# Four value columns of the MLP up-projection as block products in two units, with a shared bank and sums made by transfers

## Chip, cores and metric

The kernel runs on one core of one Trainium2 chip. The metric is the device time of one execution in microseconds (us), as the median of several runs. Engines are named as the profile names them: PE (TensorE, matmul), PEld (its weight loads), DVE (VectorE), ACT (ScalarE), POOL (GpSimd), SP (the queue from which most transfers are issued). PSUM is the memory that matmuls write; a bank is a tile of 128 x 512 f32 in this kernel.

## What is computed

Two decoder layers over 512 tokens of width 1024, in f32. Layer 0 mixes tokens by window attention and a short convolution, layer 1 by gated linear attention. Both then run the gated MLP below, which the change is about, and a per-layer embedding.

```python
D_MODEL, SEQ, D_FF, FFN_CONV_K = 1024, 512, 2816, 3

def _conv_ffn(h, w_up, conv_w, conv_b, w_down):
    u = _causal_depthwise_conv(h @ w_up, conv_w) + conv_b
    gate, up = jnp.split(u, 2, axis=-1)
    return (jax.nn.gelu(gate, approximate=False) * up) @ w_down

def reference(x, p, ...):
    for i in range(DEPTH):
        h = _rms_norm(x, mix_norm[i])
        ...
        x = x + _conv_ffn(_rms_norm(x, ffn_norm[i]), ffn_w_up[i], ffn_conv_w[i], ffn_conv_b[i], ffn_w_down[i])
        x = x + _per_layer_embedding(x, p[i], ple_norm[i], ple_w_gate[i], ple_w_proj[i])
    return x
```

`w_up` has 5632 columns: 2816 gate columns, then 2816 value columns. The convolution has three taps along the tokens.

## The kernel before

**Precision.** An f32 operand is cut into a high and a low part: ACT copies the operand in the reduced format (the high part), DVE subtracts that from the operand (the low part). A product is three matmuls: high x high, high x low, low x high. So each weight tile costs one ACT and one DVE instruction ahead of its matmuls (`cut` at L151 and L153, `cut_blocks` at L861 and L864).

**Column tiles and groups.** The up-projection is computed transposed, 128 columns of `w_up` on the partitions and 512 tokens along the bank. The 22 gate tiles and 22 value tiles of a layer are taken in 11 groups (`for d in range(groups)` in `ffn`): group d holds gate tiles 2d and 2d + 1 and value tiles 2d and 2d + 1.

**A value tile the plain way** (`value`): 8 tiles of 128 rows x 3 matmuls x 2 halves of the tokens, 48 matmuls of 256 columns (lines L177 to L179 inside `mm3`).

**Two gate tiles as block products** (`seven`, L920 on): rows by parity, columns in two tiles, and tokens in two halves form 2 x 2 blocks, and a Strassen-Winograd scheme takes seven block products in place of eight. Each is 12 matmuls (`block_product`, L916 to L918), 84 in all where two plain tiles take 96. The products are W = plain x e1, V = t13 x s1, then plain x o1, t2 x s2, t13 x s3, last x s4 and last x o2. Copies by ACT carry partial sums from one bank to another between them: W goes into the left halves of X and Y (L931, L932), V into a buffer `more` (L938), and two more copies follow (L941, L944). `seven` is a generator; the caller runs other matmuls between its steps. The scheme needs sums of blocks on both sides:
- on the weights, `first_forms` and `more_forms` make them with four DVE operations of 128 x 512 a group (L887, L888, L895, L898), in place in the loaded weights, and cut the results as `t13`, `t2` and `last`;
- on the tokens, `operand` makes s1 to s4 (L833 to L838).

**The order of a group.** PE's order is written out by hand (`manual_schedule(engines={ET.PE})`); the other engines' order comes from a scheduler that works with priorities (`high_priority`) and with explicit orderings (`issue_after`). For group d, PE runs: six eighths of the value tile 2d (`begin`), the gate's W, the rest of that value tile, V and plain x o1 and t2 x s2, the first half of value tile 2d + 1, the gate's t13 x s3, the second half of the value tile, and the gate's last two products. `prepare(d + 1)` issues the next group's loads and cuts. A group has 180 matmuls.

**Loads.** The gate weights of a group (1 MB, L1014) and the next value weights (1 MB, L990) come by SP's queue. Each has one buffer ahead only: the load for group d + 1 waits until the last cut of group d's weights (the `last` cut of `seven`) has read it.

**After the matmuls** (`taps`): DVE scales by the row norm R (L969, or L972 and L976 where `more` is added first), ACT applies the middle tap and the bias (L977), DVE the two other taps (L979, two each). Four tiles a group. Then `close`, in the next group, applies Gelu on ACT (L1130) and multiplies gate and value on DVE (L1034).

**POOL** raises the token norm to its power (`rtok`, L209), once a norm, and issues a few small loads early (L250).

**After the up phase** comes the down phase (`down`), which uses `seven` too, seven times in the whole kernel; the 22 groups of the up phases use it once each.

Of the kernel before, what the change touches and what calls it, by code (L numbers as in the profile page):

```python
# [63 lines left out]
class Kernel:  # L64
# [755 lines left out]
    def operand(self, m, gain, tags):  # L820
# [30 lines left out]
    def cut_blocks(self, src, wide=True, amid=None):  # L851
# [4 lines left out]
        else:  # L856
            h, l = (
                self.sp.tile([P, S + 64], F32R, tag="sq", name=self.nm("t2"), bufs=2)[:, o : o + S] for o in BLOCKS
            )
        h, l = (x.rearrange("p (j n) -> p j n", n=src.shape[2]) for x in (h, l))  # L860
# [5 lines left out]
        n = 2 if wide else 1  # L866
# [53 lines left out]
    def seven(self, od, ws, x, keep=None):  # L920
# [5 lines left out]
        W, V = self.pa(), self.pa()[:, :H]  # L926
        X, Y = self.ps(), self.ps()
        plain, t13, t2 = ws
        left, right = HALVES
# [4 lines left out]
        product(V, t13, 0, x["s1"], True)  # L934
# [14 lines left out]
    def ffn(self, i, project, next_gain):  # L949
# [8 lines left out]
        with tc.tile_pool(name=f"ffn{i}", bufs=1) as fp:  # L958
# [7 lines left out]
            def taps(y, ps, f, more=None, behind=None):  # L966
# [3 lines left out]
                else:  # L970
# [4 lines left out]
                    with tc.issue_after(behind.ins) if behind else nullcontext():  # L975
                        nc.vector.tensor_tensor(z, z, R, ALU.mult)  # L976
# [28 lines left out]

            def prepare(d, behind=None):
# [91 lines left out]
            with tc.manual_schedule(engines={ET.PE}):  # L1098
                late = begin(0, steps, w0c)
                close = lambda: None  # L1100
                for d in range(groups):
# [4 lines left out]
                    V1 = self.pa()  # L1106
                    value(w1c, V1, 0, ND // 2)
                    if d == 0:
                        self.end_norm()
                    copied = next(steps)  # L1110
                    value(w1c, V1, ND // 2, ND)
                    if d == 0:
                        R = self.spread()
# [1183 lines left out]
```

## Time and profile before

| what | us |
|---|---|
| median of 3 runs | 1196.59 (1196.03 to 1197.21) |
| the profiled execution | 1195.99 |
| its span | 1194.0 |
| up phase of layer 0, groups 0 to 10 | 178.4 to about 403 |
| up phase of layer 1 | from about 791.5 to 1018 |
| one group | about 20.45 |

The profile is of one execution; its rows give the start and the duration of an instruction, the engine, the line, the operation, and what it wrote from what. A note in brackets says how long the engine was idle before it, and what ended that. Where a row groups two instructions (x2), its duration covers both. Durations of DVE overlap by some 0.08 us with the next one, so its pace is read from starts. Lines as L864 are those of the kernel before.

### The profile page before, as it was taken

What the parts mean: (1) busy time and instruction counts of PE and PEld (TensorE: products, weight loads), DVE (VectorE), ACT (ScalarE), POOL (GpSimd) and SP (SyncE); (2) the same over time, 40 slices, a digit from 0 to 9 for tenths busy, and PEclk for the clock granted to TensorE, in tenths of its full rate; (3) what the DMA queues carried; (4) which work ended last, traced back from release to release, by engine and by line L of the source; (5) the groups of instructions that cost most, each with busy time, mean ns of one, the idle gap of its engine ahead of it and who ended that gap; (6) DMA issues with size and microseconds to landing.
All of it is one profiled execution on the core that took longest, in us unless ns stands there. A gap on an engine that the chain in (4) does not pass through costs nothing.

```text
span 1194.0 us, 20222 instructions
## 1 busy us (share of the span) xinstructions
PE 1187.1 (99%) x8218; PEld 1079.2 (90%) x8218; DVE 993.3 (83%) x1595; ACT 691.6 (58%) x1138; POOL 46.1 (4%) x64
## 2 busy tenths in 40 slices
PE   9999999999999999999999999999999999999998
PEld 8877789999999988889988988899999999888887
DVE  6786687898999987889879876688989999988595
ACT  7466565656565744756664655555555656655374
POOL 2610000000000000000100000000000000000000
PEclk9999999999999999999999999999999999999999
DMA  7222222333323343422412212223232333323601
GB/s 224 72 97 81 74 89 71 107 107 106 107 93 103 113 137 96 130 73 73 139 59 71 89 54 72 88 76 116 92 116 97 106 107 113 126 89 98 211 1 71
DMA packets 113072, 117.76 MB, mean 99 GB/s; under 512 B 2856, under 2 KB 108002, under 8 KB 112980
## 3 DMA queue, kind: packets, MB, share of 16 engines
q1 hardware_dynamic: 112144, 115.88, 29.8%
q8 instruction: 64, 1.05, 0.4%
q0 software_dynamic: 560, 0.42, 0.3%
q14 instruction: 28, 0.23, 0.1%
q10 hardware_dynamic: 276, 0.18, 0.1%
HBM read 114.37 MB, written 2.10 MB: 98 GB/s over the span
## 4 chain that ended last, share of the span: by engine, by line
PE 88%; DVE 8%; ACT 3%; issue 1%; DMA 0%; POOL 0%; ACTq 0%
PE ps L177 8%; PE ps L178 8%; PE ps L179 8%; PE pa L178 6%; PE pa L179 6%; PE pa L177 6%; PE ps L916 5%; PE ps L918 5%; PE ps L917 5%; PE ps L193 5%; PE ps L191 5%; PE ps L200 4%; PE pa L916 2%; PE pa L918 2%; PE pa L917 2%; DVE wl L864 2%
## 5 line engine op out<-in xcount | busy, mean ns | idle before, releaser
L153 DVE TENSOR_TENSOR wl<-raw,wh 128x1024 fp32r<-128x1024 f32 (+3 forms) x138 | 158.6, 1152 | 39.6 <-ACT wh L151 36.5
L151 ACT ACTIVATE wh<-raw 128x1024 fp32r<-128x1024 f32 (+4 forms) x142 | 140.9, 995 | 68.4 <-PE ps L178 26.3
L861 ACT ACTIVATE wh<-raw 128x1024 fp32r<-128x1024 f32 x90 | 95.7, 1063 | 129.5 <-DVE raw L888 79.0
L979 DVE SCALAR_TENSOR_TENSOR zt<-z,vfa,zt 128x510 f32<-128x510 f32 (+1 forms) x176 | 130.8, 744 | 0.3
L864 DVE TENSOR_TENSOR wl<-raw,wh 128x1024 fp32r<-128x1024 f32 x90 | 109.9, 1221 | 17.5 <-ACT wh L861 16.4
L179 PE MATMUL pa<-b,wl 128*128 128x256 f32 x352 | 97.3, 276 | 0.1
L179 PE MATMUL pa<-a,wl 128*128 128x256 f32 x352 | 97.2, 276 | 0.0
L177 PE MATMUL pa<-a,wh 128*128 128x256 f32 x352 | 97.2, 276 | 0.0
L177 PE MATMUL pa<-b,wh 128*128 128x256 f32 x352 | 97.2, 276 | 0.0
L178 PE MATMUL pa<-a,wh 128*128 128x256 f32 x352 | 97.2, 276 | 0.0
L178 PE MATMUL pa<-b,wh 128*128 128x256 f32 x352 | 97.2, 276 | 0.0
L977 ACT ACTIVATE zt<-z,vfb 128x512 f32<-128x512 f32 x88 | 71.3, 810 | 18.3 <-DVE z L969 8.7
L191 PE MATMUL ps<-b,wh 128*128 128x512 f32 (+1 forms) x192 | 73.0, 383 | 0.0
L193 PE MATMUL ps<-b,wh 128*128 128x512 f32 (+1 forms) x192 | 72.3, 379 | 0.0
L179 PEld LDWEIGHTS pa<-b,wl 128*128 128x128 f32 x352 | 66.1, 188 | 0.3 <-DVE wl L153 0.3
L177 PEld LDWEIGHTS pa<-a,wh 128*128 128x128 f32 x352 | 66.1, 188 | 0.0
L177 PEld LDWEIGHTS pa<-b,wh 128*128 128x128 f32 x352 | 66.1, 188 | 0.0
L178 PEld LDWEIGHTS pa<-b,wh 128*128 128x128 f32 x352 | 66.1, 188 | 0.0
L178 PEld LDWEIGHTS pa<-a,wh 128*128 128x128 f32 x352 | 66.1, 188 | 0.0
L179 PEld LDWEIGHTS pa<-a,wl 128*128 128x128 f32 x352 | 66.1, 188 | 0.0
L916 PE MATMUL ps<-four,wh 128*128 128x256 f32 x232 | 64.7, 279 | 0.0
L918 PE MATMUL ps<-four,wl 128*128 128x256 f32 x232 | 64.1, 276 | 0.0
(532 smaller groups left out, 3711.9 us busy)
## 6 DMA issues: line engine op xcount, KB each, us to landing
raw<-in_ffn_w_up_dram SPq DMA_DIRECT2D x42, 1024.0 KB, 5.1
raw<-in_ffn_w_down_dram SPq DMA_DIRECT2D x13, 1024.0 KB, 5.1
raw<-in_hy_w_in_dram SPq DMA_DIRECT2D x8, 1024.0 KB, 4.9
raw<-in_gla_w_in_dram SPq DMA_DIRECT2D x8, 1024.0 KB, 5.2
raw<-in_ffn_w_down_dram SPq DMA_DIRECT2D x8, 768.0 KB, 4.9
raw<-in_ple_w_gate_dram SPq DMA_DIRECT2D x6, 1024.0 KB, 6.5
raw<-in_hy_w_out_dram SPq DMA_DIRECT2D x16, 256.0 KB, 4.0
raw<-in_gla_w_out_dram SPq DMA_DIRECT2D x4, 1024.0 KB, 5.1
```

The lines of the kernel that those rows point to most:

```text
L151: nc.scalar.activation(hv, v, AF.Copy)
L153: self.rest_cut = nc.vector.tensor_tensor(lv, v, hv.bitcast(F32), ALU.subtract)
L177: mm(out, lh, rh, start=start, stop=False, **kw)
L178: mm(out, lh, rl, start=False, stop=False, **kw)
L179: mm(out, ll, rh, start=False, stop=stop, **kw)
L191: mm(out, lh, rh, start=first, stop=False, **kw)
L193: end = mm(out, lt, rt, start=False, stop=False, **kw)
L861: nc.scalar.activation(h, src, AF.Copy)
L864: nc.vector.tensor_tensor(l, src, h.bitcast(F32), ALU.subtract)
L916: mm(out, wh, xh, start=first and j == 0, stop=False, **kw)
L918: mm(out, wl, xh, start=False, stop=j == ND // 2 - 1, **kw)
L979: nc.vector.scalar_tensor_tensor(out=y[:, tap:], in0=z[:, : S - tap], scalar=w[:, f : f + 1], in1=y[:, tap:], op0=ALU.mult, op1=ALU.add,)
```

## The change

- In `ffn`, `pairs_by_blocks = (1, 4)`: in the groups d = 1 and d = 4, the value tiles 2d + 1 and 2d + 2 form a `Unit` and are computed as seven block products in place of two plain tiles. Its first products (`first`, `second`) stand in PE's order of group d where tile 2d + 1 stood; `third` and `fourth` stand in that of group d + 1 where tile 2d + 2 stood, with `third` ahead of the gate's W and `fourth` after it.
- In `seven`, and in the units, V goes into the right half of W's bank. The product that begins it does so without the start flag.
- Sums on the weight side become additions: the signs of the forms are turned, with `operand` on the token side turned to match and a factor of -1 in `taps`.
- Five sums a layer are made by transfers in `sum_ahead`: a copy of the blocks from DRAM into a tile, then two transfers that add other blocks onto it, all issued by POOL. These are the gate sums of groups 1 and 2 (issued in `prepare(0)`), of group 3 (`prepare(1)`), and the value sums of the two units (each in its own `prepare`). The other forms stay on DVE (`sum_forms`).

Functions that the new code calls and that were there before: `cut_blocks` (now with its body in `cut_into`), `block_product`, `by_parity`, `four`.

```diff
@@ operand
-            nc.vector.tensor_tensor(s12[:, :H], e[:, H:], o[:, H:], ALU.add)
-            nc.vector.tensor_tensor(s12[:, H:], s12[:, :H], e[:, :H], ALU.subtract)
+            nc.vector.tensor_tensor(s12[:, :H], o[:, H:], e[:, H:], ALU.subtract)
+            minus = lambda out, p, q: nc.vector.scalar_tensor_tensor(
+                out=out, in0=p, scalar=-1.0, in1=q, op0=ALU.mult, op1=ALU.subtract
+            )
+            minus(s12[:, H:], s12[:, :H], e[:, :H])
...
-            nc.vector.tensor_tensor(s34[:, H:], o[:, :H], s12[:, H:], ALU.subtract)
+            minus(s34[:, H:], o[:, :H], s12[:, H:])
@@ seven
-        W, V = self.pa(), self.pa()[:, :H]
+        left, right = HALVES
+        W = self.pa()
+        V = W[:, right]
...
-        product(V, t13, 0, x["s1"], True)
+        product(V, t13, 0, x["s1"])
@@ taps
-                        nc.vector.tensor_tensor(z, z, R, ALU.mult)
+                        nc.vector.scalar_tensor_tensor(
+                            out=z, in0=z, scalar=-1.0, in1=R, op0=ALU.mult, op1=ALU.mult
+                        )
@@ ffn
+            pairs_by_blocks = (1, 4)
+            ahead_of = {0: (1, 2), 1: (3,)}
+            blocks = a["ffn_w_up"][i].rearrange("(j u p) n -> u p j n", p=P, u=2)
+            gate_sums, value_sums, places = {}, {}, {}
+
+            def sum_ahead(sums, d, c):
+                key = id(sums)
+                if key not in places:
+                    x = self.four(fp, F32).rearrange("p (h a) b -> p h (a b)", h=2)
+                    places[key] = [x[:, h].rearrange("p (j n) -> p j n", n=2 * P) for h in range(2)]
+                x = sums[d] = places[key][d % 2 if sums is gate_sums else 0]
+                nc.gpsimd.dma_start(x, blocks[0, :, :, c : c + 2 * P])
+                for u in range(2):
+                    nc.gpsimd.dma_start(
+                        x[:, :, u * P : (u + 1) * P], blocks[u, :, :, c + P : c + 2 * P], accum_op=ALU.add
+                    )
+
+            def sum_forms(raw, both13, apart=False):
+                ev, od = self.by_parity(raw)
+                if apart:
+                    b11, b21, b22 = ev[:, :, :P], od[:, :, :P], od[:, :, P:]
+                    plain = self.cut_blocks(raw[:, :, :P])
+                    four = self.four(fp)
+                    h, l = (four[:, 2 * u : 2 * u + 2].rearrange("p a b -> p (a b)") for u in range(2))
+                    t13 = self.cut_into(h, l, both13)
+                    nc.vector.tensor_tensor(b11, b22, both13[:, :, :P], ALU.add)
+                    with tc.high_priority(offset=40):
+                        t2 = self.cut_blocks(b11, False)
+                    nc.vector.tensor_tensor(b21, b21, b11, ALU.add)
+                    return plain, t13, t2
+                plain = self.cut_blocks(raw[:, :, :P])
+                given = both13 is not None
+                if not given:
+                    both13 = ev
+                first, third = both13[:, :, :P], both13[:, :, P:]
+                if not given:
+                    nc.vector.tensor_tensor(first, ev[:, :, P:], ev[:, :, :P], ALU.add)
+                    nc.vector.tensor_tensor(third, od[:, :, P:], ev[:, :, P:], ALU.add)
+                t13 = self.cut_blocks(both13)
+                nc.vector.tensor_tensor(first, od[:, :, P:], first, ALU.add)
+                with tc.high_priority(offset=40):
+                    t2 = self.cut_blocks(first, False)
+                nc.vector.tensor_tensor(od[:, :, :P], od[:, :, :P], first, ALU.add)
+                return plain, t13, t2
+
+            class Unit:
+                def __init__(u, raw, ws):
+                    u.od = self.by_parity(raw)[1]
+                    u.plain, u.t13, u.t2 = ws
+                    u.more = places[id(value_sums)][1].rearrange("p j n -> p (j n)")[:, : S // 2]
+
+                def first(u):
+                    left, right = HALVES
+                    W, u.X, u.Y = self.pa(), self.pa(), self.pa()
+                    self.block_product(W[:, left], u.plain, 0, operands["e1"], True)
+                    for x in (u.X, u.Y):
+                        nc.scalar.copy(x[:, left], W[:, left])
+                    u.V = W[:, right]
+
+                def second(u):
+                    left, right = HALVES
+                    self.block_product(u.V, u.t13, 0, operands["s1"])
+                    nc.scalar.copy(u.more, u.V)
+                    self.block_product(u.X[:, left], u.plain, 1, operands["o1"])
+                    self.block_product(u.Y[:, left], u.t2, 0, operands["s2"])
+                    nc.scalar.copy(u.X[:, right], u.Y[:, left])
+                    u.last = self.cut_blocks(u.od)
+
+                def third(u):
+                    right = HALVES[1]
+                    self.block_product(u.X[:, right], u.t13, 1, operands["s3"])
+                    nc.scalar.copy(u.Y[:, right], u.X[:, right])
+
+                def fourth(u):
+                    left, right = HALVES
+                    self.block_product(u.Y[:, left], u.last, 1, operands["s4"])
+                    self.block_product(u.X[:, right], u.last, 0, operands["o2"])
@@ prepare
-                rv = values.pop()
-                with tc.issue_after(behind.ins) if behind else nullcontext():
-                    w0 = column(rv, rv.shape[2] // P - 1)
+                rv, w0 = values.pop(), None
+                if d - 1 not in pairs_by_blocks:
+                    with tc.issue_after(behind.ins) if behind else nullcontext():
+                        w0 = column(rv, rv.shape[2] // P - 1)
+                if d in pairs_by_blocks:
+                    sum_ahead(value_sums, d, DFF + 256 * d + P)
...
-                ws = self.seven_forms(ev, od, rg)
+                ws = sum_forms(rg, gate_sums.get(d))
                 values.append(load_values(d))
-                return self.seven(od, ws, operands, self.aside), w0, column(values[0], 0)
+                steps = self.seven(od, ws, operands, self.aside)
+                for e in ahead_of.get(d, ()):
+                    sum_ahead(gate_sums, e, 256 * e)
+                if d not in pairs_by_blocks:
+                    return steps, w0, column(values[0], 0)
+                rv = values[0]
+                return steps, w0, Unit(rv, sum_forms(rv, value_sums[d], True))
@@ begin
+                if isinstance(w, Unit):
+                    next(steps)
+                    w.fourth()
+                    return lambda y: taps(y[:, 0], w.Y, NF + 2 * d, w.more)
@@ the loop over groups
+                    unit = w1c if isinstance(w1c, Unit) else None
+                    if unit:
+                        unit.first()
+                        copied = next(steps)
+                        unit.second()
+                        V1 = unit.X
+                    else:
...
                     if d + 1 < groups:
                         steps, w0c, w1c = prepare(d + 1, copied)
-                        cut = self.rest_cut
+                        if unit:
+                            unit.third()
+                            w0c = unit
+                        else:
+                            cut = self.rest_cut
                         late = begin(d + 1, steps, w0c)
```

More of the change, by code (lines that the diff above doesn't have):

```diff
@@ L859, in cut_blocks, with cut_into @@
             )
+        return self.cut_into(h, l, src, amid)
+    def cut_into(self, h, l, src, amid=None):
+        nc = self.nc
+        n = src.shape[1] * src.shape[2] // S
         h, l = (x.rearrange("p (j n) -> p j n", n=src.shape[2]) for x in (h, l))
@@ L865, in cut_blocks @@
         h, l = (x.rearrange("p j n -> p (j n)").rearrange("p (k n) -> p k n", n=P) for x in (h, l))
-        n = 2 if wide else 1
         return lambda j, c: (h[:, n * j + c, :], l[:, n * j + c, :])
@@ L925, in seven @@
         product = self.block_product
-        W, V = self.pa(), self.pa()[:, :H]
+        left, right = HALVES
+        W = self.pa()
+        V = W[:, right]
         X, Y = self.ps(), self.ps()
         plain, t13, t2 = ws
-        left, right = HALVES
         product(W[:, left], plain, 0, x["e1"], True)
@@ L1105, in ffn @@
                         close()
[L1106 to L1113, printed above, removed]
+                    unit = w1c if isinstance(w1c, Unit) else None
[5 more added lines that the diff above has]
+                    else:
+                        V1 = self.pa()
+                        value(w1c, V1, 0, ND // 2)
+                        if d == 0:
+                            self.end_norm()
+                        copied = next(steps)
+                        value(w1c, V1, ND // 2, ND)
+                        if d == 0:
+                            R = self.spread()
                     X, Y, more = next(steps)
```

## The prediction

> **What bounds the kernel now.** I read the page first (busy shares, chain of waits), then busy time by windows, then the timelines of each engine around the changed groups.
>
> ```profile
> span 1194.0 us, 20222 instructions
> PE 1187.1 (99%) x8218; PEld 1079.2 (90%) x8218; DVE 993.3 (83%) x1595; ACT 691.6 (58%) x1138; POOL 46.1 (4%) x64
> PE 88%; DVE 8%; ACT 3%; issue 1%; DMA 0%; POOL 0%; ACTq 0%
> ```
>
> TensorE is never idle for long: a matmul taken out is time gained, unless something else cannot deliver earlier. Who that could be shows by windows (times; busy us and instructions of PE, weight load, DVE, ACT, POOL; clock; DMA share; GB/s):
>
> ```profile
> 301.10:321.60 20.50, 20.50 (x183) 20.50 (x183) 19.08 (x26) 12.15 (x18) 0.00 (x0) 1.00 0.32 105
> 403.40:423.80 20.40, 20.40 (x96) 17.02 (x95) 20.40 (x30) 12.20 (x16) 0.00 (x0) 1.00 0.45 143
> ```
>
> The first is one group of the up phase: DVE has 1.4 us to spare in 20.5. The second opens the down phase: DVE has none. The granted clock is 1.00, and ACT and POOL have room. So the change trades TensorE's time for work of an engine nearly as full, and for transfers.
>
> **What is removed: matmuls.** A unit is 84 matmuls in place of 96; four units save 48. Their pace, from the starts of the first matmul of a block product and of the one after its twelfth:
>
> ```profile
> 224.25 0.28 PE L916 MATMUL pa<-a,wh 128*128 128x256 f32 x1
> ...
> 225.61 0.28 PE L177 MATMUL pa<-a,wh 128*128 128x256 f32 x1
> ```
>
> 12 in 1.36 us, 0.1133 each: 48 x 0.1133 = 5.44 us, 2.72 a layer, 1.36 a unit. The rest asks how late TensorE runs against that schedule. A stall at one place gives the other engines the same time, so the latenesses below are not added within a layer: the largest counts.
>
> **Two products in one bank.** V may now start only when ACT has copied W out twice; in before it had a bank of its own. The second copy and V's first matmul, in the layer's first group and in a steady one:
>
> ```profile
> 185.09 0.33 ACT L932 COPY ps<-pa 128x256 f32<-128x256 f32 x1
> ...
> 185.22 0.28 PE L916 MATMUL pa<-four,wh 128*128 128x256 f32 x1
> ...
> 287.68 0.36 ACT L932 COPY ps<-pa 128x256 f32<-128x256 f32 x1
> ...
> 288.57 0.28 PE L916 MATMUL pa<-four,wh 128*128 128x256 f32 x1
> ```
>
> First group: the copy ends at 185.42, so V is 0.20 late, some 0.25 with a hand-over. Steady: it ends 0.53 ahead, cost nothing; without that cover each of the other groups would pay a part of the copies' 0.62.
>
> **The plain product comes earlier after a unit.** Where a unit ended the group, the next group begins with its plain gate product, without the 36 matmuls of a value column ahead of it, only the unit's third product: 24 matmuls, 2.72 us, sooner. What that product waits for in group 2 of layer 0 is DVE's lower half of the gate weights:
>
> ```profile
> 220.54 1.22 DVE L864 TENSOR_TENSOR wl<-raw,wh 128x1024 fp32r<-128x1024 f32 x1
> ...
> 224.48 0.28 PE L918 MATMUL pa<-a,wl 128*128 128x256 f32 x1
> ```
>
> Ready at 221.76, used at 224.48: 2.72 of slack, and the need moves to just 221.76. Now what goes before it. The load starts when group 1's last cut frees the buffer:
>
> ```profile
> 199.51 0.68 DVE L887 TENSOR_TENSOR raw<-raw 128x512 f32<-128x512 f32 x1
> 200.11 0.68 DVE L969 TENSOR_TENSOR z<-pa,R 128x512 f32<-128x512 f32 x1
> ...
> 203.77 0.75 DVE L979 SCALAR_TENSOR_TENSOR zt<-z,vfa,zt 128x510 f32<-128x510 f32 x1
> 204.43 0.69 DVE L895 TENSOR_TENSOR raw<-raw 128x512 f32<-128x512 f32 x1
> ...
> 211.75 1.22 DVE L864 TENSOR_TENSOR wl<-raw,wh 128x1024 fp32r<-128x1024 f32 x1
> ...
> 212.99 0.37 SPq L1014 DMA_DIRECT2D raw<-in_ffn_w_up_dram  x1
> ...
> 218.99 1.05 ACT L861 ACTIVATE wh<-raw 128x1024 fp32r<-128x1024 f32 x1
> DMA to landing us min/median/max: 4.8/5.0/6.4
> ```
>
> By starts, a 512-wide operation takes 0.60 of DVE and a scaled one 0.66. From the first z of group 1 to that cut, the built order has 23 DVE instructions where before had 20: two gate sums leave, two of the unit's and its t2 cut come, and more taps stand ahead; in all three scaled ones more, +1.98. The sign flips themselves swap a 0.60 for a 0.66, counted in this. Cut 214.95, load +5.0 = 219.97, ACT +1.05, DVE +1.22 = 222.25: late by 0.5, plus what the load loses to the sums' transfers (c).
>
> **c.** The 1 MB load now runs beside unit 4's sum. No row shows an accumulating transfer; the nearest are these (the last line is of POOL's vector loads, 22 KB):
>
> ```profile
> 133.14 1.52 POOL L250 DMA_DIRECT2D vrow<-in_ffn_conv_w_dram  x3 [56.35 <-PE pa L259]
> raw<-in_ffn_w_up_dram SPq DMA_DIRECT2D x42, 1024.0 KB, 5.1
> zt<-in_ffn_w_down_dram SPq DMA_DIRECT2D x6, 512.0 KB, 4.2
> pin<-in_p_dram SPq DMA_DIRECT2D x4, 256.0 KB, 3.6
> DMA to landing us min/median/max: 1.8/2.3/4.9
> ```
>
> 512 KB more costs 5.1 - 4.2 = 0.9. The 512 KB that accumulate beside the load cost nothing if they miss it, and three times that, 2.7, if source, old value and result each count; I take c = 1.0, the price of one passage.
>
> **The sums' own path.** The base copy of group 3's gate sum may start when group 1's t2 cut has read its place (198.91 + 6.74 = 205.7 by the count above). An issue is 0.51; landing I take from SP's rows. Base lands 205.7 + 0.5 + 4.2 = 210.4; POOL waits for it, issues two accumulates (211.4), then unit 4's base, whose place unit 1 gave up at 210.6: lands 216.1; accumulates issued 217.1, landed 220.7. Their reader, ACT's and DVE's cut for unit 4's t13, stands early in the built order: ahead of group 2's t2 cut (0.64) and of the two copies (0.63) that V needs.
>
> ```profile
> 226.97 0.28 PE L916 MATMUL pa<-four,wh 128*128 128x256 f32 x1
> ```
>
> V is due 1.36 earlier than this plus 0.25, at 225.9, so the sum is due at 225.9 - 0.63 - 0.64 - 1.06 = 223.5: 2.8 us of margin, and past it every us is a us of TensorE. Unit 1's sum and the gate sums of groups 1 and 2 have more:
>
> ```profile
> 172.96 1.29 DVE L110 TENSOR_TENSOR four<-four,four 128x512 fp32r<-128x512 f32 x2 [1.08 <-ACT four L109]
> ...
> 189.12 1.23 DVE L864 TENSOR_TENSOR wl<-raw,wh 128x1024 fp32r<-128x1024 f32 x1 [1.46 <-ACT wh L861]
> 193.64 1.04 POOL L209 TENSOR_TENSOR rtok<-rs,mhalf 128x4 f32<-128x4 f32 x1 [58.48 <-DVE rs L208]
> ```
>
> Its place is free at 174.3; base and accumulates land by some 184, its cut comes behind that of 189.12, and POOL is done issuing long before the norm's rtok. Without that cover, rtok, and with it the whole first group's scaling, waits.
>
> On these sums the Trainium skill ("SBUF — State Buffer", section "SBUF: two separate sides") warns that descriptors which GpSimd writes for a DMA are held up while DVE runs an operation in a two-port mode; by that rule the sums would come late as in rival 2. The three POOL loads of 133.14, issued in 0.51 us each, do not bear it out. Its page "DMA: Bandwidth & Descriptors" (section "Anatomy of one DMA — SWDGE (gpsimd) path") gives 2.0 us + bytes / 436e3 for such a DMA; by that estimate the sum lands near 217 and rival 2 has twice the margin to cross.
>
> **Unit 4.** In group 4 the built order puts the Gelu ahead of ACT's copies of the unit's W, and V of the unit waits for those:
>
> ```profile
> 216.88 1.29 DVE L1034 TENSOR_TENSOR u<-zt,zt 128x512 f32<-128x512 f32 x2 [2.47 <-ACT zt L1130]
> ...
> 256.25 1.29 DVE L1034 TENSOR_TENSOR u<-zt,zt 128x512 f32<-128x512 f32 x2 [1.19 <-ACT zt L1130]
> ...
> 272.25 0.28 PE L177 MATMUL pa<-a,wh 128*128 128x256 f32 x1
> ...
> 273.28 1.53 DVE L979 SCALAR_TENSOR_TENSOR zt<-z,vfa,zt 128x511 f32<-128x511 f32 x2
> ...
> 274.90 1.06 ACT L1130 ACTIVATE zt<-zt 128x1024 f32<-128x1024 f32 x1 [1.55 <-DVE zt L979]
> ```
>
> The Gelu is released by the tap that ends at 274.81. Since 198.91 DVE has 0.9 us less to do by then (seven 512-wide fewer, five scaled more). Its idle times before were 2.47, 1.19 and 1.19 = 4.85; now cuts cover one Gelu and part of another (1.35, 0.1, 1.19), and it waits 1.1 + c for the load: 3.75 + c. Release 274.81 - 0.9 - 1.1 + c = 272.8 + c; Gelu, two copies, +1.8: V at 274.6 + c. Due: the unit starts where the old column did (272.25), V 24 matmuls later, less the first unit's gain: 272.25 + 2.72 - 1.36 = 273.6. Late by 1.0 + c = 2.0, the largest of the layer (group 5's load, 2.7 later for DVE's backlog, comes out 0.3 + c late).
>
> **Sum.** 1195.99 - 5.44 + 2 x 2.0 = 1194.55 for the profiled execution (2.0 outside the span, left alone). The runs' median, 1196.59, is 0.60 above it: **1195.1 us**. With c = 0 and no Gelu wait (0.5 a layer) 1192.2; with c = 2.7 it is 1198.5: the forecast's own range.
>
> **Rivals.**
> (1) Nothing is late: the load misses the transfers and DVE gets ahead. For it: PE 99% with 1.4 us of DVE spare. Against: DVE has three operations more ahead of the load. 1195.99 - 5.44 + 0.60 = 1191.2.
> (2) The sums land late, slower than before: place, unit 4's t13 cut in front of group 2's t2 and W copies in both layers. At 1.7 times the landing times assumed (7.1 and 6.1) the path ends 205.7 + 0.5 + 7.1 + 1.0 + 0.5 + 7.1 + 1.0 + 6.1 = 229.0, 5.5 late: 1195.99 - 5.44 + 11.0 + 0.6 = 1202.2; at twice, 1209. It takes over past 225.5 (2.0 late), and ends above before's time past 226.2. For it: POOL's landings reach 4.9 for 22 KB, accumulating was never seen, and DVE is busy. Against: 2.8 us margin.
> (3) DVE becomes the bound: its 2.7 of backlog after unit 4 is not worked off (0.2 a group beyond the Gelu's 1.19) and meets the full window of the down phase. 2.7 + 1.0 late a layer: 1198.6.
> (4) Bank sharing costs in every group: the 0.53 of cover speaks against; 0.3 in 20 more groups gives 1201. Too unlikely for a share of its own.
>
> **Chances.** Forecast 0.44 (0.17 of it below 1194.2), rival 1 0.17, rival 2 0.27, rival 3 0.12 (0.06 of it above 1199.0). A measurement of this kernel can tell some 0.2%, 2.4 us, from no change. Faster 0.17 + 0.17 = 0.34; slower 0.27 + 0.06 = 0.33; same 0.33. The range goes from rival 1 to most of rival 2: 1191.2 to 1201.5.
>
> **What would show it.** Matmuls 48 fewer; a stall of TensorE near 0.2 before the first group's V; in group 2 a wait of 1 to 2 us for the plain weights with the load's landing above 5.0; in group 4 one behind the Gelu; unit 4's accumulates landed near 221. Accumulates landing after 226, or DVE without idle time through groups 5 to 10, would make it wrong to the slow side; no waits at all, to the fast.

## The result, and the profile after

The changed kernel takes 1218.1 us (median of 4 runs, 1216.1 to 1218.62) where the kernel before takes 1196.9 on the same chip: ratio 1.0173, 95% interval 1.0155 to 1.0191. It is slower by 1.7%, 23.0 us above the forecast and outside its range. The profiled execution took 1216.1; its span is 1214.3, 20.3 more than before.

From the page of the changed kernel: the span, the engines' busy time, the chain that ended last by engine, and three rows of DMA issues (count, KB each, median us from issue to landing).

```profile
span 1214.3 us, 20267 instructions
PE 1192.9 (98%) x8170; PEld 1080.3 (89%) x8170; DVE 1001.8 (83%) x1603; ACT 701.5 (58%) x1166; POOL 80.0 (7%) x94
PE 72%; DVE 12%; DMA 6%; issue 6%; ACT 4%; POOL 1%; ACTq 0%; POOLq 0%; DVEq 0%; SPq 0%
raw<-in_ffn_w_up_dram SPq DMA_DIRECT2D x42, 1024.0 KB, 5.0
four<-in_ffn_w_up_dram POOLq DMA_DIRECT2D x10, 512.0 KB, 4.6
four<-in_ffn_w_up_dram POOLq DMA_DIRECT2D x20, 256.0 KB, 6.6
```

PE has its 48 matmuls fewer, but is 5.8 us longer busy, and its idle time grew from 1194.0 - 1187.1 = 6.9 to 21.4. DMA, at 0% of the chain before, now holds 6%. The transfers of 256 KB, the ones that add, land later than the copies of twice their size. The balance of the span: -5.44 for the matmuls taken out, +14.5 of idle PE, and 5.8 + 5.44 = +11.2 because the matmuls that are left keep PE busy for longer; together +20.3.

The idle time by what it waited for (view of PE's waits of the changed kernel: us in total, times, longest):

```profile
PE pa L924 <- ACT wh L870: 4.5, 3, 2.4
PE pa L924 <- ACT ps L941: 4.3, 4, 2.2
PE pa L926 <- DVE wl L873: 2.8, 5, 0.8
PE pa L924 <- ACT pa L1090: 2.1, 2, 1.4
PE ps L924 <- ACT ps L950: 1.0, 2, 0.8
```

Row by row: the plain weights' cut, the copy of W that V waits for in a gate, the lower half of the same weights, the unit's copy that follows its third product, and a copy further on in the scheme of a gate. The median load (5.0) hides it, as a median does: only a few loads are late, those beside the sums and, in group 5 of layer 0, a gate load and a value load beside each other (some 7 us each). Where the time goes shows by windows (times; busy us and count of PE, weight load, DVE, ACT, POOL; clock; DMA share; GB/s), here groups 2 and 5 of layer 0 and all behind group 6 up to the end of that up phase:

```profile
219.30:239.70 20.40, 15.62 (x103) 15.02 (x102) 11.90 (x16) 8.32 (x12) 2.37 (x2) 0.83 0.48 111
...
280.60:301.00 20.40, 17.76 (x145) 16.91 (x145) 14.97 (x20) 10.84 (x19) 0.00 (x0) 1.00 0.31 104
...
321.40:410.00 88.60, 88.60 (x780) 88.40 (x779) 83.63 (x112) 52.06 (x76) 0.00 (x0) 1.00 0.31 100
```

In the first, PE is idle for 4.8 and does 103 matmuls where a full window holds 180; 103 at 0.1133 would be 11.7, not 15.6, so 3.9 more are lost around the waits and to slower matmuls, at a granted clock of 0.83 in the mean. Behind group 6 nothing is lost any more.

Group 2 of layer 0 by rows: first POOL, then DVE and SP's queue, then ACT, then PE (start, us, engine, line, operation; in brackets how long the engine was idle, and what ended that).

```profile
210.23 2.60 POOL L1030 DMA_DIRECT2D four<-in_ffn_w_up_dram  x2 [3.32 <-DMA four<-in_ffn_w_up_dram]
211.75 1.86 POOL L1028 DMA_DIRECT2D four<-in_ffn_w_up_dram  x1
219.09 2.58 POOL L1030 DMA_DIRECT2D four<-in_ffn_w_up_dram  x2 [5.48 <-DMA four<-in_ffn_w_up_dram]
...
213.73 1.22 DVE L873 TENSOR_TENSOR wl<-raw,wh 128x1024 fp32r<-128x1024 f32 x1
215.02 0.37 SPq L1108 DMA_DIRECT2D raw<-in_ffn_w_up_dram  x1
...
222.76 1.06 ACT L870 ACTIVATE wh<-raw 128x1024 fp32r<-128x1024 f32 x1 [3.99 <-DMA raw<-in_ffn_w_up_dram]
...
230.93 1.06 ACT L870 ACTIVATE four<-four 128x1024 fp32r<-128x1024 f32 x1 [5.89 <-DMA four<-in_ffn_w_up_dram]
231.89 0.61 ACT L870 ACTIVATE t<-four 128x512 fp32r<-128x512 f32 x1
232.41 0.36 ACT L940 COPY ps<-pa 128x256 f32<-128x256 f32 x1
232.71 0.33 ACT L941 COPY ps<-pa 128x256 f32<-128x256 f32 x1
```

Group 1's last cut ends at 214.95, and the load leaves at 215.02, just as forecast. But it lands at 222.74, after 7.7 us. Beside it go the second of gate 3's accumulates (landed 217.40; the first landed at 215.00, before the load left), unit 4's base (issued 211.75, landed 218.81, after 7.1) and, from 219.1 on, the next value load and unit 4's accumulates. These land at 229.31 and 230.82. ACT has been idle for 5.89 us by then: its next instruction is the t13 cut of that sum, and the t2 cut and both copies of W stand behind it, all of them with their data ready.

```profile
223.87 0.38 PE L924 MATMUL pa<-a,wh 128*128 128x256 f32 x1 [1.85 <-ACT wh L870]
224.09 0.28 PE L925 MATMUL pa<-a,wh 128*128 128x256 f32 x1
225.13 0.39 PE L926 MATMUL pa<-a,wl 128*128 128x256 f32 x1 [0.76 <-DVE wl L873]
...
226.42 0.41 PE L924 MATMUL pa<-four,wh 128*128 128x256 f32 x1
...
229.41 0.41 PE L926 MATMUL pa<-a,wl 128*128 128x256 f32 x1
...
233.09 0.50 PE L924 MATMUL pa<-four,wh 128*128 128x256 f32 x1 [2.17 <-ACT ps L941]
```

Two waits of PE follow, for the load and for the sum. Between 226.42 and 229.41 stand 14 steps of a matmul in 2.99 us, 0.213 each in place of 0.113. From 233.39 on, behind the second wait, comes another such stretch.

### The profile page after: what moved, and what is told of

Its sections match the earlier page's. It is cut to its first block, busy times and chain, and to the rows that moved or that the text cites. A ratio compares the mean times of both kernels' runs of the same rounds, so it can differ in the third digit from the quotient of the medians.

```text
span 1214.3 us, 20267 instructions
## 1 busy us (share of the span) xinstructions
PE 1192.9 (98%) x8170; PEld 1080.3 (89%) x8170; DVE 1001.8 (83%) x1603; ACT 701.5 (58%) x1166; POOL 80.0 (7%) x94
## 4 chain that ended last, share of the span: by engine, by line
PE 72%; DVE 12%; DMA 6%; issue 6%; ACT 4%; POOL 1%; ACTq 0%; POOLq 0%; DVEq 0%; SPq 0%
PE ps L177 8%; PE ps L178 8%; PE ps L179 7%; PE ps L193 4%; PE ps L191 4%; DMA four<-in_ffn_w_up_dram 4%; PE ps L200 4%; PE ps L924 4%; PE ps L926 4%; PE ps L925 4%; PE pa L178 3%; PE pa L179 3%; PE pa L177 3%; DVE wl L873 3%; DVE zt L990 2%
## 5 line engine op out<-in xcount | busy, mean ns | idle before, releaser
L153 DVE TENSOR_TENSOR wl<-raw,wh 128x1024 fp32r<-128x1024 f32 (+3 forms) x130 | 149.2, 1150 | 36.3 <-ACT wh L151 33.7
L990 DVE SCALAR_TENSOR_TENSOR zt<-z,vfa,zt 128x511 f32<-128x511 f32 (+1 forms) x176 | 129.9, 747 | 1.6 <-ACT zt L988 1.1
L179 PE MATMUL pa<-b,wl 128*128 128x256 f32 x288 | 79.7, 277 | 0.1
L179 PE MATMUL pa<-a,wl 128*128 128x256 f32 x288 | 79.6, 276 | 0.0
L177 PE MATMUL pa<-b,wh 128*128 128x256 f32 x288 | 79.5, 276 | 0.0
L178 PE MATMUL pa<-b,wh 128*128 128x256 f32 x288 | 79.5, 276 | 0.0
L177 PE MATMUL pa<-a,wh 128*128 128x256 f32 x288 | 79.5, 276 | 0.0
L178 PE MATMUL pa<-a,wh 128*128 128x256 f32 x288 | 79.5, 276 | 0.0
L924 PE MATMUL ps<-four,wh 128*128 128x256 f32 x232 | 64.9, 280 | 1.0 <-ACT ps L950 1.0
L925 PE MATMUL ps<-four,wh 128*128 128x256 f32 x232 | 64.1, 276 | 0.0
L179 PEld LDWEIGHTS pa<-b,wl 128*128 128x128 f32 x288 | 54.1, 188 | 0.3 <-DVE wl L153 0.2
L177 PEld LDWEIGHTS pa<-b,wh 128*128 128x128 f32 x288 | 54.1, 188 | 0.0
L178 PEld LDWEIGHTS pa<-b,wh 128*128 128x128 f32 x288 | 54.1, 188 | 0.0
L177 PEld LDWEIGHTS pa<-a,wh 128*128 128x128 f32 x288 | 54.1, 188 | 0.0
L178 PEld LDWEIGHTS pa<-a,wh 128*128 128x128 f32 x288 | 54.1, 188 | 0.0
```

Source lines behind the costliest of these rows:

```text
L153: self.rest_cut = nc.vector.tensor_tensor(lv, v, hv.bitcast(F32), ALU.subtract)
L177: mm(out, lh, rh, start=start, stop=False, **kw)
L178: mm(out, lh, rl, start=False, stop=False, **kw)
L179: mm(out, ll, rh, start=False, stop=stop, **kw)
L924: mm(out, wh, xh, start=first and j == 0, stop=False, **kw)
L925: mm(out, wh, xl, start=False, stop=False, **kw)
```

## Experiments

Line numbers are those of the changed kernel; each diff is against it unless the text names another base.

**Hold unit 4's cut back.** The t13 cut of unit 4 is ordered behind ACT's copy of the gate in hand, so that it can't stand in front of group 2's work.

```diff
-                    t13 = self.cut_into(h, l, both13)
+                    with tc.issue_after(behind.ins) if behind else nullcontext():
+                        t13 = self.cut_into(h, l, both13)
```

> Unit 4's t13 cut is queued on ACT behind group 3's copy, so that nothing of group 2 stands behind the late sum; its transfers run as in the changed kernel. Theory (the wait for the sum in front of group 2's t2 cut and W copies costs its 2.17 and 1.30 us of stall and most of the slow clock after it): those two stalls go, the group 2 load stays late (1.85 and 2.41), 1216.1 falls by 6 to 10, to 1206 to 1210. Rival (DVE's extra work is the bound): other stalls grow in their place, at 1214 or above.

1209.3, ratio 1.0108 (1.0093 to 1.0123): 8 us of the 21 are gone, as expected. V's wait in group 2 is gone in both layers; the wait for the load stays (2.05 + 0.75 in layer 0). So the head of ACT's queue was the one cause, the late load another.

**Another place for unit 4's sum.** It goes to a tile that comes free after group 3's t2 cut, so its transfers move from group 2 to group 4.

```diff
+                if sums is value_sums and d == 4:
+                    x = places[id(gate_sums)][1]
```

> Unit 4's sum goes into the place of group 3's gate sum, which comes free some 35 us later, so its transfers leave groups 1 and 2 altogether. Theory (late sum, and contention on group 2's load, 7.7 and 8.3 us to landing in place of 5.0): load back at 5.0 to 5.5, stalls in group 2 below 0.7 a layer, the stalls in groups 5 and 6 stay: 1216.1 less 16 of group 2 plus 1, 1199 to 1203. Rival (the load is late of itself, DVE's backlog): stall in group 2 stays above 1.5 a layer, 1206 or above.

1225.4, ratio 1.024: a miss, the sum is late in the new place as well. POOL, then ACT in group 4 of layer 0:

```profile
253.03 0.78 POOL L1031 DMA_DIRECT2D four<-in_ffn_w_up_dram  x1 [39.30 <-DVE t L873]
257.24 2.57 POOL L1033 DMA_DIRECT2D four<-in_ffn_w_up_dram  x2 [3.43 <-DMA four<-in_ffn_w_up_dram]
...
267.74 1.06 ACT L870 ACTIVATE four<-four 128x1024 fp32r<-128x1024 f32 x1 [8.66 <-DMA four<-in_ffn_w_up_dram]
```

The base lands after 3.9 (POOL issues again at 257.24), the first accumulate 4.7, and the second, of which the greater part runs beside the load of the next gate, 9.6 (258.01 to 267.64). That load takes 9.1 itself (issued 259.12). PE waits 6.1 us behind the same cut, in one piece. And group 2's load is still late, by gate 3's accumulates alone (7.9 from issue to landing).

**The shared bank alone**, in the kernel before.

```diff
-        W, V = self.pa(), self.pa()[:, :H]
+        W = self.pa()
+        V = W[:, H:]
...
-        product(V, t13, 0, x["s1"], True)
+        product(V, t13, 0, x["s1"])
```

> The kernel before with V in the right half of W's bank and nothing else. Theory (only the first group of a layer pays): 0.2 to 0.25 a layer, 1196.3 to 1197.2. Rival (sharing costs in each of 29 sets of block products): 3 us or more, 1199 or above.

1197.6, ratio 1.0005 (0.9996 to 1.0014). One wait of 0.2 before the first group's V, none elsewhere: nothing, where ACT is on time.

**Without units**, with the gate sums still made by transfers.

```diff
-            pairs_by_blocks = (1, 4)
+            pairs_by_blocks = ()
```

> The changed kernel without units: gate sums of groups 1 to 3 by transfers, turned signs, shared bank. Theory (transfers cost only where something urgent stands behind them): their landings have room, DVE is freed of six sums a layer: 1195.5 to 1197.5. Rival (accumulating transfers on POOL's queue slow the weight loads wherever they run): stalls of 1 us or more in groups 1 to 3, 1200 or above.

1198.1, ratio 1.0016 (1.0002 to 1.0029), a little above what was expected. Gate 3's accumulates alone stretch group 2's load to 8.5 us (issued 212.14, landed 220.61), and V of that group waits 1.2 to 1.4. Three gate sums a layer off DVE have bought nothing.

**The held cut, and another order of PE.** On top of the first experiment, the units' third and fourth products go between the gate's last two, so that W comes later and the load has more time.

```diff
+        if halt:
+            yield
...
+                    if unit:
+                        next(steps)
+                        unit.third()
...
+                    if unit:
+                        unit.fourth()
```

> On top of e1 (unit 4's cut held back, 1209.3): the unit's third and fourth are put between the gate's last two products, so that the next group's W comes after all of them, 24 matmuls later, where it stood in the kernel before. Theory (W comes too early for a load that lands late; the waits of 2.05 + 0.75 and 1.90 + 0.76 and the slow clock after them come from that): both go below 0.5, 1198 to 1202. Rival (DVE's backlog is what is waited for, wherever W stands): new waits in groups 2 and 5 of the same size, 1206 or above.

1211.8, ratio 1.012: a miss. The load is no earlier, and now the unit's fourth product waits 1.9 to 2.0 for a copy that stands on ACT behind the cut that waits for the load. The backlog is waited for wherever the product stands, as the rival had it.

**All sums on DVE**, no transfers. (`more` gets a tile of its own.)

```diff
-            ahead_of = {0: (1, 2), 1: (3,)}
+            ahead_of = {}
...
-                return steps, w0, Unit(rv, sum_forms(rv, value_sums[d], True))
+                return steps, w0, Unit(rv, sum_forms(rv, None))
```

> The changed kernel with no transfer sums at all: DVE makes the gate sums as before and both sums of each unit in place; units, order, bank and signs stay. Theory (transfers cost by what waits for them and by slowing the loads; units cost little): no sum is late and the load lands in 5.0 to 5.5, but DVE has some 6 us a layer more, so the load of group 2 starts 1 to 2.5 later than in the changed kernel: 1202 to 1210. Rival (transfers are the whole cost): 1196 or below. Rival (DVE is the bound of the units in any form): 1214 or above.

1228.4, ratio 1.0257: a miss, far above what was expected and where the second rival had it. The load of group 2 takes 5.2 us now, near its 5.0 of elsewhere, so the transfers were what stretched it. But it leaves 4.5 later than in the changed kernel (219.52), since DVE gets to the last cut later, and the waits for cuts and copies, 22.7 us by the view of PE's waits, spread over groups 1 to 7. Without the transfers DVE is the bound, at a higher price.

**A stall by itself.** In the kernel with the shared bank alone, ACT copies W ten times more in group 2 of each layer; no transfer is added.

```diff
-        nc.scalar.copy(Y[:, left], W[:, left])
+        for _ in range(1 + again):
+            nc.scalar.copy(Y[:, left], W[:, left])
```

> e3 (1197.6), with ACT repeating the second copy of W ten times in group 2 of each layer, so that V starts some 2.2 us late there and nothing else is changed. Rival (a stall costs its own length): 1201 to 1203. Theory (after a stall of about 2 us TensorE's clock is granted lower for a while, as the windows of the changed kernel show it at 0.65 to 0.80, and the loss is about double): 1204 to 1209, with granted clock below 0.9 in the windows behind it.

1212.5, ratio 1.0119. The stall came out longer than meant, 5.86 a layer, as other work of ACT fell in between. Its cost is 8.5 and 8.0 a layer, by the start of the group's t2 product against before. The wait in layer 0 and the windows behind it:

```profile
233.75 0.58 PE L916 MATMUL pa<-four,wh 128*128 128x256 f32 x1 [5.86 <-ACT ps L934]
...
232.00:236.00 4.00, 2.25 (x10) 2.25 (x11) 3.00 (x5) 2.30 (x6) 0.00 (x0) 0.51 0.00 0
236.00:240.00 4.00, 4.00 (x25) 4.00 (x24) 0.00 (x0) 1.31 (x2) 0.00 (x0) 0.63 0.02 4
240.00:244.00 4.00, 4.00 (x38) 4.00 (x37) 2.52 (x3) 1.45 (x3) 0.00 (x0) 1.00 0.31 96
```

The clock falls to 0.51 and 0.63 and is back at 1.00 after some 6 us: 2.1 to 2.7 us lost beyond the stall, with no transfer of sums in the kernel. (The whole profiled execution is 14.9 longer than that of the shared bank alone, which leaves 1.6 a layer.) So a stall alone brings slower matmuls; transfers are not needed for them. This stall is over twice as long as any wait of the changed kernel, so for those it is not shown by this run; where their slow matmuls lie is told below.

**All sums early.** Both units' sums are issued ahead of group 1 (in layer 0 from 174.81 on), into a half tile each; group 3's gate sum goes back to DVE.

```diff
-            ahead_of = {0: (1, 2), 1: (3,)}
+            ahead_of = {0: (1, 2)}
...
-                x = sums[d] = places[key][d % 2 if sums is gate_sums else 0]
+                x = sums[d] = places[key][d % 2 if sums is gate_sums else d // 4]
...
-                if d in pairs_by_blocks:
-                    sum_ahead(value_sums, d, DFF + 256 * d + P)
+                if d == 1:
+                    for e in pairs_by_blocks:
+                        sum_ahead(value_sums, e, DFF + 256 * e + P)
```

> The changed kernel with unit 4's sum moved ahead of group 1 beside unit 1's (in a place of its own; the copy of V goes where group 1's gate sum was) and group 3's gate sum made by DVE, so that no transfer sum runs from 195 us on. Theory (the group 2 load is late because accumulates run beside it): it lands in 5.0 to 5.5, W waits 0.5 to 1.0 in group 2, the waits of groups 4 to 6 stay: 1199 to 1205. Rival (the load's lateness is DVE's alone): 1207 or above, like e1.

1205.7, ratio 1.0071 (1.0056 to 1.0086), 0.7 above what was expected, 12 us below the changed kernel. Group 2's load takes 5.6 us (215.69 to 221.28), and that group, which lost 9, runs level with before. What is left lies in groups 4 to 6, where no sum is in flight: group 5 of layer 0, ACT and SP.

```profile
277.77 0.37 SPq L1109 DMA_DIRECT2D raw<-in_ffn_w_up_dram  x1
280.27 0.37 SPq L1001 DMA_DIRECT2D raw<-in_ffn_w_up_dram  x1
...
284.65 1.06 ACT L870 ACTIVATE wh<-raw 128x1024 fp32r<-128x1024 f32 x1 [2.92 <-DMA raw<-in_ffn_w_up_dram]
288.51 1.06 ACT L870 ACTIVATE wh<-raw 128x1024 fp32r<-128x1024 f32 x1 [2.80 <-PE pa L926]
289.48 0.37 ACT L1090 COPY pa<-pa 128x256 f32<-128x256 f32 x1
289.78 0.33 ACT L940 COPY ps<-pa 128x256 f32<-128x256 f32 x1
290.04 0.35 ACT L941 COPY ps<-pa 128x256 f32<-128x256 f32 x1
```

The gate load leaves late, as DVE ends the last cut only at 277.31, and takes 6.9 with the value load 2.5 us behind it; then the copies of unit and gate stand behind cuts on ACT.

**The queues cleared too.** On top of that: the held cut, the other order of PE, the last cut pulled ahead on DVE, group 5's gate cuts ordered behind the unit's copy on ACT, and the value cut asked for after W.

```diff
+        with self.tc.high_priority(offset=200) if halt else nullcontext():
+            last = self.cut_blocks(od)
...
+                with tc.issue_after(unit.copied.ins) if unit else nullcontext():
+                    ws = sum_forms(rg, gate_sums.get(d))
```

> e8 (1205.7) with the queues cleared around the units: third and fourth between the gate's last two products as in e5; on ACT the next group's gate cuts behind the copy that follows third; unit 4's t13 cut behind group 3's copy; the gate's last cut raised in both units' groups so that the next gate load starts earlier; the next value cut asked for after the gate's W. Theory (what is left in e8 is head-of-line waiting on ACT and a load that starts late): the waits of groups 2, 5 and 6 fall below 0.5 each, 1193 to 1198. Rival (DVE cannot carry unit 4 at all): waits of about the same sum elsewhere, 1203 or above.

1205.8, ratio 1.0071: a miss. The loads are on time now (276.95 to 281.86 in group 5), and only one kind of wait is left of size. From the views of PE's waits of this kernel:

```profile
PE pa L924 <- ACT ps L941: 8.3, 9, 1.4
```

V waits for ACT's copies of W, four times a layer (the ninth wait is the 0.2 of the first group); the wait has moved to the place where the shared bank makes PE depend on ACT.

**Unit 1 alone**, on top of the early sums.

```diff
-            pairs_by_blocks = (1, 4)
+            pairs_by_blocks = (1,)
```

> e8 without the unit at group 4 (24 matmuls saved, 2.7 us). Theory (e8's loss is unit 4's, which has its sums and cuts on a DVE with 1.4 us to spare a group, and a gate load that shares with the value load): all waits from group 4 on vanish, one of 0.7 in group 2 stays: 1195 to 1198. Rival (every unit costs): above 1199.

1196.11 (11 runs, 1195.33 to 1196.88), ratio 0.999 (0.9981 to 0.9998), as expected. Of the new waits one is left, 0.8 in group 2 of layer 0. Unit 4 thus costs 0.0081 of 1197, 9.7 us, in a kernel with all sums early, the 2.72 that its matmuls save already taken off, and unit 1 with its two gate sums brings about 1 us of the 2.72 that its matmuls are worth. Of the kernels that leave nothing out it is the only one that ends below the one before, by 0.1%, less than what a measurement of this kernel was said to tell from no change.

**The same with cleared queues** (the edits of two runs above).

> e9 without the unit at group 4. Theory: as e10 with the wait of 0.7 in group 2 gone too, 1193.5 to 1196.5, the first version that may end below the kernel before. Rival (the raised cut and the held-back cuts only move the wait): as e10 or above.

1199.6, ratio 1.0019: clearing costs 3.5 us here, V waits 1.43 + 0.68 in layer 0 and 1.44 + 0.92 in layer 1. The rival was right.

**V in a bank of its own again**, in the changed kernel, in the one with cleared queues, and in the one with unit 1 alone. In these three a part of the units' sums is lost, so only their times are read. This would fit what the Trainium skill ("PSUM — Partial Sum Buffer", section "The four PSUM rules") states, that a matmul with the start flag clears the marks of what has been written over its whole bank: a unit that later uses the other half of that bank adds onto a copy made by ACT, without a start flag, and would overwrite it. It was not tried by itself.

```diff
-        V = W[:, right]
+        V = self.pa()[:, :H]
...
-        product(V, t13, 0, x["s1"])
+        product(V, t13, 0, x["s1"], True)
```

> The changed kernel with the gates' V in a bank of its own again; units, transfers and signs stay. Theory (the shared bank turns a late ACT copy into a wait 12 matmuls, 1.36 us, sooner): each wait before V (2.17, 1.43, 1.30, 0.68, 0.60) loses up to 1.36, in all 4 to 6 and part of the slow clock: 1208 to 1213. Rival (the copies are so late that the place of V does not matter): 1215 or above.

> e9 with the gates' V in a bank of its own. Theory: its waits of 1.43, 0.68, 0.56 and 1.36 a layer before V vanish or fall below 0.2: 1205.8 falls to 1195 to 1199. Rival (the waits pass on to the next product, plain x o1, which needs the same copies): 1203 or above.

> e10 (1196.1) with the gates' V in a bank of its own. Theory: 0.2 a layer in the first group, 1195.2 to 1196.2. Rival (the bank that the unit then lacks makes another wait): 1197 or above.

1213.5, ratio 1.0137 (1.0123 to 1.0151), between the two theories, nearer the first; 1201.4, 1.0036 (1.0023 to 1.005), between them too; and 1195.49, 0.9986 (0.9977 to 0.9994), as expected. Against the same kernels with the shared bank that is 0.0036, 0.0035 and 0.0004 less: some 4 us where ACT is late, 0.5 where it is not. Even so, the one with two units and cleared queues stays above before. PE's waits in it:

```profile
PE ps L924 <- ACT ps L950: 3.0, 2, 1.5
PE pa L926 <- DVE wl L873: 2.3, 3, 0.8
```

The waits for V are gone, and the next copy of ACT and the lower half of the weights from DVE come late instead: the two engines' backlog after unit 4 is the bound, and the bank decides where it is paid and adds some 4 us.

## Why the prediction was wrong

**What is removed** was right: 48 matmuls, 5.44 us. But a matmul removed moves the needs of all that follow forward, and DVE, ACT and the transfers did not follow.

**Two products in one bank** was right by itself (a wait of 0.18 in the first group for the 0.25 forecast, nothing elsewhere in the kernel with the bank alone). The cover of 0.53 that it leaned on was named as its condition, and the units take it away: the bank then costs some 4 us.

**The plain product comes earlier** was right to 0.1 us up to the load's issue (last cut done 214.95, load issued 215.02), and wrong behind it by c.

**c** was taken as 1.0 and measured 7.7 - 5.0 = 2.7, at the upper end of the bounds, in layer 0; in layer 1 the same load took 8.3, so 3.3, outside them. The wait followed, 1.85 + 0.76 and 2.41 + 0.75. The taken value failed, not the mechanism that a load beside the sums is late: the forecast had unit 4's sum alone beside it, and 256 KB of gate 3's sum and the next value load were in flight too. With the sums elsewhere the load takes 5.6, without any 5.2.

**The sums' own path is the step that failed.** Gate 3's base was right (4.2 taken; 206.08 to 209.94 is 3.9). Unit 4's, beside an accumulate and the load, took 7.1 for the same 4.2. The accumulates' 3.6 was read from SP's rows of plain transfers of 256 KB. In the changed kernel they took these times (source view of that line):

```profile
L1030 POOL DMA_DIRECT2D four<-in_ffn_w_up_dram x20: 1269/1810/2836, 143.7 to 846.5; - x20
  ACT four L870: 10.6, 2
DMA to landing us min/median/max: 4.7/6.6/11.0
```

Not one of the 20 came near 3.6; the median is 6.6, and unit 4's two, beside gate load and value load, took 10.2 and 11.0. The middle row is the price: for these ACT sat idle for 10.6 us, in two pieces, one a layer. Unit 4's sum was to land at 220.7 with 2.8 us of margin, and landed at 230.8, 7.3 past its due time; past 226 was named as a sign of being wrong to the slow side. (The second estimate, given as near 217, comes out at 217.9 by the forecast's own steps and is further off.) The order was foreseen: rival 2 gave the place, the cut in front of group 2's t2 and W copies, and the point from which it decides (225.5); its price was worked out at 1.7 and 2 times the landing times, and the accumulates took nearly 3 times theirs. Of PE's 14.5 us of idle time, 3.5 are the waits behind this cut in both layers and 5.8 those for the load beside the sums; nearly all the rest lies in groups 4 to 6. Holding the cut back removes the first (8 us in the time) and moving all sums early nearly both (12 us; 0.70 is left in group 2 of layer 0).

**The largest counts** failed as well. The forecast did not add the latenesses of a layer, since a stall gives the other engines the same time. In layer 0 of the changed kernel group 2 stalls for 4.8 and groups 4 to 6 for 2.9 more. The kernel with early sums, where group 2 stalls for 0.7 alone, has 3.6 there; in layer 1 it has 2.6 for 2.4. The two kernels also differ in group 3's sum, which is on DVE in the second; as far as they compare, a stall of over 4 us took 0.2 to 0.7 off the later ones, and the latenesses add nearly in full.

**A term that was missing: the clock.** The sum counted a late microsecond as a microsecond. Of the 25.7 us that stand against the 5.44, 11.2 are longer busy time. Part is around each wait, and not in its bracket: from 294.25, the last matmul before the wait of 1.43 in group 5, to the second after it, 296.19, are 1.94 us, where 1.43 and two steps of 0.113 make 1.66; 0.28 more, some 4.5 us for the 16 waits of both up phases. Another part is matmuls at 0.213, in three stretches of 3.4 us at half the clock. These are the two of layer 0, each with the 3.4 us before it (windows as above); below them is one of the kernel with early sums:

```profile
223.00:226.40 3.40, 1.77 (x12) 1.57 (x13) 2.52 (x3) 2.04 (x3) 0.00 (x0) 1.00 1.13 226
226.40:229.80 3.40, 3.40 (x18) 3.40 (x17) 0.54 (x1) 0.00 (x0) 0.00 (x0) 0.50 0.65 88
229.80:233.20 3.40, 1.23 (x11) 1.03 (x9) 1.19 (x2) 2.27 (x5) 0.00 (x0) 1.00 0.02 2
233.20:236.60 3.40, 3.40 (x17) 3.40 (x18) 3.40 (x6) 2.34 (x3) 0.00 (x0) 0.50 0.00 0
...
286.50:289.90 3.40, 1.45 (x11) 1.25 (x11) 2.15 (x4) 1.39 (x3) 0.00 (x0) 1.00 0.01 3
289.90:293.30 3.40, 3.40 (x16) 3.40 (x17) 2.97 (x4) 1.11 (x3) 0.00 (x0) 0.50 0.00 0
```

The third is in layer 1, from 851.0 to 854.4, with 13 matmuls. Together 48 matmuls at 0.1 more each make 4.8 us. The 2 us that remain of the 11.2 were not traced to a place. With the measured idle time and busy time in place of the forecast's 4.0, the sum is 1195.99 - 5.44 + 14.5 + 11.2 = 1216.25, against 1216.1; this only closes the balance, as both were read from this execution.

**Unit 4** was wrong in its place. The Gelu ahead of W's copies made no wait there; group 4 has 0.21 and 0.82 at a later copy (L950), and the kernel with early sums has 0.84 and 0.86, also there. Group 5 was taken as the lesser (0.3 + c) and is the greater in layer 0: 0.25 + 0.76 + 1.43, and 0.27 + 0.75 + 1.43 with early sums (in layer 1 it has 0.68 and 0.76, less than group 4). c there is no accumulate, but the value load beside the gate load (6.8 to 6.9 for 5.0), since DVE's backlog brings the gate load to it; and the backlog on ACT behind it was not counted at all.

**The other rivals.** Rival 1 fell with the first wait. Rival 3 is borne out in direction: once the sums are early, DVE's and ACT's backlog after unit 4 is what is left, at 9.7 us with the saved matmuls taken off, where the rival had 2 x 3.7 before that; it does not reach the down phase, as the window behind group 6 of layer 0 is full. Rival 4 holds only where the cover is gone.

What stays open: how the 9.7 of unit 4 divide between DVE and ACT, as no run gives one of them time without the other; and why a transfer that adds takes longer than a copy of twice its size. A busy DVE alone did not hold a transfer of POOL's up: DVE was busy without a pause from 206.08 to 209.94, and the plain copy issued there landed in 3.9.

## What to carry to other kernels

A transfer that adds onto its destination has to be measured before it is planned with, and beside which loads: here it cost its own lateness and that of the load next to it. An instruction that waits for a transfer should never be placed early in an in-order queue that a critical engine depends on. When PE is full and DVE has 7% to spare, matmuls taken out are worth little, and the waits that they uncover cost more than their length: 14.5 us of idle time came with 11.2 of longer busy time here, two stalls of 5.9 on purpose with 3.2 to 4.8 beyond their length.

## What was not expected of the hardware

- Accumulating transfers of 256 KB took 4.8 and 6.3 us with no load beside them and up to 11.0 beside loads of 1 MB, and gate loads of 1 MB took 7.4 to 9.1 beside them in these runs, for 5.0. Plain copies of 512 KB by the same queue took 3.9 to 4.2 in the changed kernel where nothing ran beside them.
- By the starts of its rows (210.23, 211.00, 211.75) POOL issued a copy or an accumulate every 0.77 us, where its small loads took 0.51 each.
- Waits of 1.85 and 0.76 us, with two matmuls between them, were followed within 1.3 us by matmuls at 0.213 in place of 0.113. The granted clock was 0.50 for stretches of 3.4 us (twice that behind the stall of 5.86), and in the 3.4 us before each of the three shown above PE was busy for 1.2 to 1.8. Nearly the same waits did either: 0.25, 0.76 and 1.43 in group 5 of layer 0 left the clock at 1.00, and 0.27, 0.75 and 1.43 in the same group of the kernel with early sums brought it to 0.50 for one such stretch. The Trainium skill ("TensorE: Matmul & The Clock Gate", section "What's actually happening") gives an idle window of about 3.4 us as what halves the clock. The half and the 3.4 us agree with this trace. That the window is idle does not: no wait of the changed kernel was longer than 2.4, and the 3.4 us before its first slow stretch held 12 matmuls; the measurement decides.
